# Gated S5/pooling step: chunk groups of 64, 64, 69, 69 for 69, 69, 64, 64, and two shared PSUM banks for the state-space products

## Chip, core and metric

The kernel runs on one core of one Trainium2 chip. The metric is device time in microseconds (us) of one execution; shorter is better.

## The reference, cut to what matters

Prompt (16 meta tokens and 2,048 new ones) and sample (8 sequences of 8 tokens) go through one hybrid layer, all in float32:

```
xn   = rmsnorm(h, norm_gain)
u_s, z_s, u_p, z_p, gates = split(xn @ w_in)           # six blocks of 1024
y_s  = S5 state-space branch of u_s: per group of 16 channels a complex diagonal
       recurrence s[t] = abar*s[t-1] + bbar*u[t] (64 states), y = Re(c*s) + d*u,
       gelu, then y * sigmoid(y @ w_glu + b_glu)
y_p  = causal window means (2, 4, 8, 16) of u_p minus u_p, mixed per window group
merged = g_s * ((y_s * silu(z_s)) @ w_branch_ssm) + g_p * ((y_p * silu(z_p)) @ w_branch_pool)
out  = rmsnorm(h + merged @ w_out, final_norm_gain)
```

The final states of both branches are outputs too.

## The kernel before, in words

**Tiling.** Features lie on the 128 partitions (8 blocks of 128), tokens along the free axis. T = 8 consecutive tokens are a chunk; 258 prompt chunks and 8 sample chunks make 266. They are cut into four groups (`GROUPS`) of 69, 69, 64 and 64 chunks, g0 to g3. A group has C = 8 x chunks columns, 552, 552, 512, 512. In g0 two of the chunks hold the meta tokens; only the units `us` and `up` work on them (`meta=True`), all other units of g0 have D = 536 columns. A group over 512 columns is worked in two halves (`nh` = 2), since a matmul's output is at most 512 columns wide.

**Units.** A unit is one 128 x 1024 weight block against one group (`proj`). Each float32 operand is split into a high and a low part; for each of 8 k steps a unit issues three matmuls (`mm3`, lines 129, 131 and 133: high by high, high weight by low operand, low weight by high operand) for each half: 24 matmuls of 512 columns where `nh` is 1, 48 of 268 or 276 where it is 2. ACT makes the high part of each weight block (L106) and DVE the low part (`wl`, L207) two units ahead. What is done with a unit's result (`post`) runs one unit later on ACT and DVE.

**Order of the units.** Written out by hand: us of g1 (8 units), us of g0 (8), u_pool of g0 (8 up, 8 zp, 3 gates, 4 half-sized mixes), u_pgate of g0 (13), zs of g0 (3), us of g2 (8), zs of g0 (2), us of g3 (8), zs of g0 (3), two gates, then u_rest of g0 (glu, split of the product `a`, gate, brs, gates, out), then for g1, g2 and g3 each u_pool, u_pgate, zs and u_rest. Beside the first 39 units runs the preparation of the state-space matrices (`BESIDE`: `params`, then `batches`): DVE, POOL, ACT and some small PE work, the tiles bt, ct, ps_bt and ps_k, at fixed places between matmuls.

**State-space branch.** The products run on 32 pairs of channel groups in two rounds: round 0 over the chunks of g0 and g1 (138), round 1 over those of g2 and g3 (128). A tick advances a software pipeline by one pair: its EARLY steps are issued a quarter of the way into a unit (or a part of it), its LATE steps at the end. On tick n, EARLY has st_out of pair n-6 (ACT reads `sy`, SP stores `ys`), st_turn_a and st_turn_v of pair n-2 (ACT and DVE read `sx`), st_swap, st_turn_g, st_state (POOL), st_phase, st_wrap, st_mat (SP loads `smc`); LATE has st_sin, st_rot, st_scan, st_y of pair n-5 (PE writes `sy` from `su`, `sS`, `smc`), st_x of pair n-1 (PE writes `sx` from `su`, `smb`) and st_load (SP). `sx` and `sy` are one PSUM tile each, so that st_x of a pair must wait until the reads of the pair before it, in the same tick's EARLY, are done; likewise st_y.

`spread` places the 38 ticks of a round evenly over a range of units, with a lower share in units named `busy`: round 0 from the start of u_pgate of g0 to the end of us of g3, round 1 from the glu of g0 to the end of u_pgate of g2. `a_split` of all 8 feature blocks (4 or 8 in one unit) follows the last glu of a group: 8 DVE subtractions on L115 one behind the other.

In round 1 the last 8 columns are the sample sequences; their start states are loaded beside `su` in st_load and copied by POOL into `sS` in st_state.

All DMAs are issued by SP, in program order.

Of the kernel before, what the change touches and what calls it, by code (L numbers as in the profile page):

```python
# [20 lines left out]
P = 128  # L21
DM = 1024
NB = DM // P
T = 8
KP = (2048 + 16) // T
NS = 8
# [8 lines left out]
RK = (2.0 * DM) ** (2.0 / 3.0)  # L35


GROUPS = [(0, 69), (69, 69), (138, 64), (202, 64)]
GOFF = [T * k0 for k0, _ in GROUPS]

ROUNDS = [(0, 138), (138, 128)]


W_US, W_ZS, W_UP, W_ZP, W_GS, W_GP, W_GLU, W_BRS, W_BRP, W_OUT = range(0, 80, 8)
# [45 lines left out]
def hybrid_step(ctx, tc, a):  # L90
# [388 lines left out]
    def two(q):  # L479
        return slice(2 * q, 2 * q + 2)  # L480
# [3 lines left out]
        return rows.rearrange("(q c) t k -> (c t) q k", q=2)  # L484

    def st_load(g, q):
        x = stile("su", 5, g.kn + (NS if g.last else 0))
        u = x[:, :, :g.kn]
        for i in (2 * g.i, 2 * g.i + 1):
            k = GROUPS[i][0] - ROUNDS[g.i][0]  # L490
            SY.dma_start(u[:, :, k:k + GROUPS[i][1]], chans(us_d[i], q))
        if g.last:
            SY.dma_start(x[:, :, g.kn:], a["s0"][:, 0, two(q)])
        mb = stile("smb", 2, P)
        SY.dma_start(mb, mat_d[q, :, 0])
        pr[q].update(u=u, mb=mb, s0=x[:, :, g.kn:])

    def st_phase(g, q):
        ph, n = stile("sph", 4), stile("scc", 4)
# [17 lines left out]
    def st_x(g, q):  # L517

        d = pr[q]
        d["px"] = sw["sx"][:, :, :g.kn]  # L520
        for j in range(2):
            PE.matmul(d["px"][:, j], d["mb"][:, j], d["u"][:, j], start=True, stop=True)  # L522

# [51 lines left out]
    def st_state(g, q):  # L575

        d = pr[q]
        c, w, kp = d["c"], d["s"], g.kp
        s = stile("sS", 3, g.kn)
        now = state[:, two(q)].unsqueeze(2)  # L580
        if g.last:
            G.tensor_copy(s[:, :, kp:], d["s0"])
        G.tensor_copy(s[:, :, 0:1], now)
        G.tensor_tensor(s[:, :, 1:kp], c[:, :, 1:kp], w[:, :, 1:kp], ALU.subtract)
        G.tensor_tensor(now, c[:, :, kp:kp + 1], w[:, :, kp:kp + 1], ALU.subtract)
        d["S"] = s

    def st_y(g, q):
        d = pr[q]
        d["py"] = sw["sy"][:, :, :g.kn]  # L590
        for j in range(2):
            m = slice(j * P, (j + 1) * P)
            PE.matmul(d["py"][:, j], d["m"][:, 0, m], d["u"][:, j], start=True, stop=False)  # L593
            PE.matmul(d["py"][:, j], d["m"][:, 1, m], d["S"][:, j], start=False, stop=True)  # L594
# [40 lines left out]
    class Group:  # L635
# [42 lines left out]
        def proj(self, w, xh, xl, halves=None, meta=False):  # L678


            ps = self.acc()
            n = self.HD if halves else self.ND
            nk = len(xh)
            for k in range(nk):
                between(k / nk)
                outs, xs = [], []
                for h in halves or range(self.nh):
                    m = n + (T * self.km if meta and h else 0)
                    outs.append(ps[:, h, :m])
                    xs.append([v[k][:, h * n:h * n + m] for v in (xh, xl)])  # L690
                mm3(outs, [x[:, k * P:(k + 1) * P] for x in w], xs, k == 0, k == nk - 1)
            return ps
# [63 lines left out]
        def rms_sum(self, ss, halves=None, early=False):  # L756

            n = self.HD if halves else ss.shape[1] // self.nh
            if early:
                ps = [psb.tile([P, 512], F32, tag=t, name=t)[:, :n] for t in ("bx", "by")]  # L760
            else:
                acc = self.acc()
                ps = [acc[:, h, :n] for h in range(self.nh)]
            for h in halves or range(self.nh):
                PE.matmul(ps[h], onesm, ss[:, h * n:(h + 1) * n], start=True, stop=True)  # L765
            self.ps = ps
# [54 lines left out]
        def up_post(self, fb, ps):  # L821
# [6 lines left out]
                es = E[:, :, 2 + kp:].rearrange("p t (s k) -> p t s k", k=3)  # L828
                G.tensor_copy(es[:, :, :, 0:2], self.hs.pop(fb))
            if last:  # L830
                src = ps[:, 0, :self.N].rearrange("p (t k) -> p t k", k=kn)
                A.activation(E[:, :, 2:2 + kp], src[:, :, :kp], AF.Copy)
                A.activation(es[:, :, :, 2:3], src[:, :, kp:].unsqueeze(3), AF.Copy)
            else:
                for dst, src in self.parts(E[:, :, 2:2 + kp], ps):
                    A.activation(dst, src, AF.Copy)  # L836
# [243 lines left out]
    grp = [Group(i) for i in range(NG)]  # L1080
    rounds = [Round(i) for i in range(len(ROUNDS))]
    units, events, parts, ticks, late = [], {}, {}, {}, {}

    def at(i, f, *args):
        events.setdefault(max(i, 0), []).append((f, args))
# [59 lines left out]
    def u_rest(g, nxt, ahead):  # L1145

        for f in range(NB):
            i = add("w", W_GLU + f, g.glu, f)
        for f in range(NB):
            at(i + 1 + (f // 4 if ahead == 0 else 0), g.a_split, f)  # L1150
        for f in range(ahead, 3 if ahead else 2):
            add("w", W_GS + f, g.gate, f, 0)
        ahead = 3 if ahead else 2
        for f in range(NB):
            b = add("w", W_BRS + f, g.brs, f)
            if nxt:
                at(b, nxt.x_load, f)
            if f >= NB - 2:
                at(b + 1, g.m_split, f)
            if f + ahead < NB:  # L1160
                i = add("w", W_GS + f + ahead, g.gate, f + ahead, 0)
                if f + ahead == NB - 1:
                    last_gs = i
        for j in range(NB - 2):
            at(max(last_gs + 1 + j // 3, 0), g.m_split, j)


        n = NB if nxt else NB - 3
        for f, h in [(f, None) for f in range(n)] + [(f, h) for h in range(2) for f in range(n, NB)]:
            i = add("w", W_OUT + f, g.out, f, h)  # L1170
            at(i - 2, g.r_load, f, g.cols(h))
            if nxt:
                if f == 0:
                    at(i, nxt.rs_load)
                if f >= 2 and f < 6:
                    at(i, nxt.x_norm, 2 * f - 4)
                    at(i, nxt.x_norm, 2 * f - 3)
        if nxt:
            at(i + 2, g.norm)
            for k in range(NB):  # L1180
                at(i + 3 + k, g.final, k)
            return
        at_part(i - 2, 0.5, lambda: g.rms_sum(g.ss, [0]))
        at_part(i - 2, 1.0, lambda: g.rms(g.ss, [0]))
        for k in range(NB):
            at(i - 1 + (0, 0, 0, 1, 1, 2, 2, 2)[k], g.final, k, 0)
            if k in LAST_GAIN:
                at(i, g.last_gain, k)
        at_part(i, 1.0, g.last_sum)
        at(i + 2, g.last_norm)  # L1190
        at(i + 3, g.last_final)

    def spread(r, lo, hi, busy, low):

        share = [low if i in busy else 1.0 for i in range(lo, hi)]
        total, done, n = sum(share), 0.0, 0
        for i, w in zip(range(lo, hi), share):
            done += w
# [25 lines left out]
    def to_ssm():  # L1224
        while beside():
            pass
        sw["g"] = ctx.enter_context(tc.tile_pool(name="gp", bufs=1))
        sw["p"], sw["end"] = pool("sw")
        ps = ctx.enter_context(tc.tile_pool(name="ps", bufs=1, space=PSUM))
        for n in ("sx", "sy"):  # L1230
            sw[n] = ps.tile([P, 2, 160], F32, name=n)

    def end_ssm():
        final_states()
# [225 lines left out]
```

## Time and profile before

| | |
|---|---|
| median of 3 runs | 2083.03 us (2082.71 to 2084.15) |
| the profiled execution | 2081.01 us, of which the span from first to last instruction is 2079.2 us |
| PE busy | 2041.4 us, 98% of the span, 13,024 matmuls |
| DVE, ACT, POOL busy | 1315.7, 1002.8, 547.7 us (63%, 48%, 26%) |
| PE share of the chain that ended last | 73% |
| mean granted TensorE clock | 0.996 |

The busy shares are means over stages with different limits. PE's clock is at its full level in nearly all of the span, so the time is the length of PE's stream of matmuls and of its waits.

### The profile page before, as it was taken

What the parts mean: (1) busy time and instruction counts of PE and PEld (TensorE: products, weight loads), DVE (VectorE), ACT (ScalarE), POOL (GpSimd) and SP (SyncE); (2) the same over time, 40 slices, a digit from 0 to 9 for tenths busy, and PEclk for the clock granted to TensorE, in tenths of its full rate; (3) what the DMA queues carried; (4) which work ended last, traced back from release to release, by engine and by line L of the source; (5) the groups of instructions that cost most, each with busy time, mean ns of one, the idle gap of its engine ahead of it and who ended that gap; (6) DMA issues with size and microseconds to landing.
All of it is one profiled execution on the core that took longest, in us unless ns stands there. A gap on an engine that the chain in (4) does not pass through costs nothing.

```text
span 2079.2 us, 33846 instructions
## 1 busy us (share of the span) xinstructions
PE 2041.4 (98%) x13024; PEld 1852.7 (89%) x13024; DVE 1315.7 (63%) x1848; ACT 1002.8 (48%) x1597; POOL 547.7 (26%) x716
## 2 busy tenths in 40 slices
PE   8999999999999999999999999999999999999998
PEld 8999899978999999999999998888888888888887
DVE  7789958898645776555764686535534676354444
ACT  5335469877446553366575653333432433243322
POOL 1156516574411430022332340012200200021001
PEclk9999999999999999999999999999999999999999
DMA  5446657587534643245445544334333443343233
GB/s 204 140 127 182 177 168 213 159 244 199 154 96 146 172 134 119 97 124 137 120 121 153 166 137 140 97 119 144 107 117 117 138 148 102 101 130 103 92 106 97
DMA packets 230466, 288.16 MB, mean 139 GB/s; under 512 B 115872, under 2 KB 160544, under 8 KB 230304
## 3 DMA queue, kind: packets, MB, share of 16 engines
q1 hardware_dynamic: 230304, 285.99, 45.9%
q8 instruction: 103, 1.69, 0.3%
q14 instruction: 59, 0.48, 0.1%
HBM read 242.61 MB, written 40.95 MB: 136 GB/s over the span
## 4 chain that ended last, share of the span: by engine, by line
PE 73%; DVE 1%; ACT 0%; DMA 0%; issue 0%; DVEq 0%; POOL 0%; ACTq 0%; POOLq 0%
PE acc L131 24%; PE acc L133 24%; PE acc L129 24%; PE sy L593 1%; PE sy L594 1%; PE sx L522 1%; DVE al L115 0%; DMA ys<-sS 0%; PE acc L765 0%; ACT wh L106 0%; DVE xr L1070 0%; DVE G L999 0%; DVE sg L998 0%; DVE wl L207 0%; DVE G L1017 0%
## 5 line engine op out<-in xcount | busy, mean ns | idle before, releaser
L129 PE MATMUL acc<-ah,wh 128*128 128x276 f32 (+4 forms) x3864 | 1047.5, 325 | 7.8 <-DVE po L798 3.3
L131 PE MATMUL acc<-al,wh 128*128 128x276 f32 (+4 forms) x3864 | 1040.7, 323 | 1.4 <-DVE al L115 0.7
L133 PE MATMUL acc<-ah,wl 128*128 128x276 f32 (+4 forms) x3864 | 1037.2, 322 | 1.2 <-DVE wl L207 1.2
L106 ACT ACTIVATE wh<-raw 128x1024 fp32r<-128x1024 f32 (+1 forms) x336 | 347.1, 1034 | 797.0 <-PE acc L131 502.9
L129 PEld LDWEIGHTS acc<-ah,wh 128*128 128x128 f32 x3864 | 647.6, 189 | 70.5 <-issue 4.4
L131 PEld LDWEIGHTS acc<-al,wh 128*128 128x128 f32 x3864 | 648.6, 189 | 58.2 <-DVE al L115 1.4
L133 PEld LDWEIGHTS acc<-ah,wl 128*128 128x128 f32 x3864 | 646.1, 188 | 55.3 <-DVE wl L207 1.8
L207 DVE TENSOR_TENSOR wl<-raw,wh 128x1024 fp32r<-128x1024 f32 (+1 forms) x336 | 420.8, 1253 | 126.9 <-ACT wh L106 126.3
L545 POOL TENSOR_TENSOR sXw<-sXw,sph 128x276 f32<-128x276 f32 (+1 forms) x64 | 50.1, 783 | 337.3 <-ACT sXw L531 337.2
L889 DVE SCALAR_TENSOR_TENSOR H<-H,acc 128x512 f32<-128x512 f32 (+2 forms) x64 | 44.9, 702 | 79.5 <-ACT H L888 79.5
L987 DVE SCALAR_TENSOR_TENSOR H<-po,H 128x512 f32<-128x512 f32 (+2 forms) x32 | 23.5, 733 | 113.3 <-ACT po L985 113.3
L115 DVE TENSOR_TENSOR al<-H,ah 128x512 fp32r<-128x512 f32 (+2 forms) x104 | 78.8, 790 | 14.9 <-ACT ah L106 14.0
L541 DVE TENSOR_TENSOR sX<-sx,scc 128x276 f32<-128x276 f32 (+1 forms) x64 | 27.0, 421 | 94.4 <-ACT sX L534 69.2
L963 POOL TENSOR_SCALAR w<-w 128x512 f32<-128x512 f32 (+2 forms) x32 | 28.7, 898 | 214.0 <-ACT w L962 213.8
L106 ACT ACTIVATE ah<-H 128x512 fp32r<-128x512 f32 (+2 forms) x88 | 50.9, 602 | 55.9 <-DVE H L919 39.6
L553 DVE TENSOR_TENSOR_SCAN sX<-r,state,sX 128x138 f32<-128x138 f32 (+1 forms) x128 | 73.0, 611 | 2.3
L1028 POOL TENSOR_TENSOR ss<-ss,po 128x512 f32<-128x512 f32 (+2 forms) x25 | 41.5, 1661 | 116.7 <-ACT po L1024 102.8
L853 DVE TENSOR_TENSOR w<-E 128x497 f32<-128x497 f32 (+2 forms) x32 | 23.6, 739 | 70.5 <-ACT E L836 49.5
L940 DVE SCALAR_TENSOR_TENSOR G<-sg,acc 128x512 f32<-128x512 f32 (+2 forms) x32 | 22.4, 701 | 72.0 <-PE acc L133 69.8
L844 POOL COPY hist<-E 128x16 f32<-128x16 f32 x24 | 14.1, 585 | 201.2 <-ACT E L836 201.0
L104 POOL TENSOR_SCALAR ah<-G 128x512 fp32r<-128x512 f32 (+2 forms) x16 | 15.1, 948 | 182.4 <-DVE sg L998 146.4
L998 DVE SCALAR_TENSOR_TENSOR sg<-sg,acc 128x512 f32<-128x512 f32 (+2 forms) x32 | 22.4, 700 | 63.1 <-PE acc L133 63.1
(239 smaller groups left out, 2203.9 us busy)
## 6 DMA issues: line engine op xcount, KB each, us to landing
raw<-in_wb SPq DMA_DIRECT2D x318, 512.0 KB, 3.6
smc<-mat_d SPq DMA_DIRECT2D x64, 256.0 KB, 3.6
smb<-mat_d SPq DMA_DIRECT2D x64, 128.0 KB, 2.6
H<-in_xb SPq DMA_DIRECT2D x22, 256.0 KB, 4.0
xr<-in_xb SPq DMA_DIRECT2D x19, 256.0 KB, 3.8
H<-in_xb SPq DMA_DIRECT2D x16, 276.0 KB, 5.3
us<-po SPq DMA_DIRECT2D x16, 276.0 KB, 4.3
su<-us SPq DMA_DIRECT2D x64, 69.0 KB, 3.1
```

Source lines behind the costliest of these rows:

```text
L106: A.activation(out, in_, AF.Copy)
L115: V.tensor_tensor(l, x, h.bitcast(F32), ALU.subtract)
L129: PE.matmul(out, wh, xh, start=first, stop=False)
L131: PE.matmul(out, wh, xl, start=False, stop=False)
L133: PE.matmul(out, wl, xh, start=False, stop=last)
L207: V.tensor_tensor(l[:, c], r[:, c], h[:, c].bitcast(F32), ALU.subtract)
L541: V.tensor_tensor(d["x"], d["px"][:, :, :g.kp], d["c"][:, :, 1:g.kp + 1], ALU.mult)
L545: G.tensor_tensor(d["xw"], d["xw"], d["s"][:, :, 1:g.kp + 1], ALU.mult)
L553: V.tensor_tensor_scan(x[:, j], r8[:, i].to_broadcast([P, g.kp]), x[:, j], state[:, i], ALU.mult, ALU.add)
L889: V.scalar_tensor_tensor(self.v3(out), self.v3(out), 1.0, self.pv(ps), ALU.add, ALU.mult)
L963: G.tensor_scalar(q, q, 0.044715, 1.0, ALU.mult, ALU.add)
L1028: (G if h is None else V).tensor_tensor(self.ss[:, c], self.ss[:, c], s, ALU.add)
```

## The change

Four things change. The groups are 64, 64, 69, 69 chunks, so that g0 and g1 have 512 columns (g0 496 without the meta chunks; `nh` = 1) and g2 and g3 have 552 (`nh` = 2); round 0 then has 128 chunks, round 1 138. The two PSUM tiles become two banks: in round 0 a pair's x and y products share bank q mod 2, so that consecutive pairs use different banks; in round 1 bank 0 holds x and bank 1 holds y, as before. Units at which a_split is issued (`full`) get no tick. The sample's start states are loaded by DMA straight into `sS` in st_state, and POOL's copy goes. The rest adapts places that assumed which groups have halves.

```diff
-GROUPS = [(0, 69), (69, 69), (138, 64), (202, 64)]
+GROUPS = [(0, 64), (64, 64), (128, 69), (197, 69)]
-ROUNDS = [(0, 138), (138, 128)]
+ROUNDS = [(0, 128), (128, 138)]
...
     def st_load(g, q):
-        x = stile("su", 5, g.kn + (NS if g.last else 0))
-        u = x[:, :, :g.kn]
+        u = stile("su", 5, g.kn)
...
-        if g.last:
-            SY.dma_start(x[:, :, g.kn:], a["s0"][:, 0, two(q)])
...
+    def bank(g, q, y):
+        if g.kn <= P:
+            return sw["b"][q % 2][:, 2 * y:2 * y + 2, :g.kn]
+        return sw["b"][y].rearrange("p (j a) k -> p j (a k)", j=2)[:, :, :g.kn]
...
-        d["px"] = sw["sx"][:, :, :g.kn]
+        d["px"] = bank(g, q, 0)
...
         if g.last:
-            G.tensor_copy(s[:, :, kp:], d["s0"])
+            SY.dma_start(s[:, :, kp:], a["s0"][:, 0, two(q)])
...
-        d["py"] = sw["sy"][:, :, :g.kn]
+        d["py"] = bank(g, q, 1)
...
-                    m = n + (T * self.km if meta and h else 0)
+                    m = n + (T * self.km if meta and h == self.nh - 1 else 0)
...
             if last:
-                src = ps[:, 0, :self.N].rearrange("p (t k) -> p t k", k=kn)
-                A.activation(E[:, :, 2:2 + kp], src[:, :, :kp], AF.Copy)
-                A.activation(es[:, :, :, 2:3], src[:, :, kp:].unsqueeze(3), AF.Copy)
+                tn = T // self.nh
+                for h in range(self.nh):
+                    ts, src = slice(h * tn, (h + 1) * tn), ps[:, h, :self.N].rearrange("p (t k) -> p t k", k=kn)
+                    A.activation(E[:, ts, 2:2 + kp], src[:, :, :kp], AF.Copy)
+                    A.activation(es[:, ts, :, 2:3], src[:, :, kp:].unsqueeze(3), AF.Copy)
...
         for f in range(NB):
             at(i + 1 + (f // 4 if ahead == 0 else 0), g.a_split, f)
+            full.add(i + 1 + (f // 4 if ahead == 0 else 0))
...
-        share = [low if i in busy else 1.0 for i in range(lo, hi)]
+        share = [0.0 if i in full else low if i in busy else 1.0 for i in range(lo, hi)]
...
-        for n in ("sx", "sy"):
-            sw[n] = ps.tile([P, 2, 160], F32, name=n)
+        sw["b"] = [ps.tile([P, 4, P], F32, name=f"sb{i}") for i in range(2)]
```

## Rows read from the trace of the kernel before

**Rows 1.** The page's head and busy times: us, share of the span, instructions.

```profile
span 2079.2 us, 33846 instructions
...
PE 2041.4 (98%) x13024; PEld 1852.7 (89%) x13024; DVE 1315.7 (63%) x1848; ACT 1002.8 (48%) x1597; POOL 547.7 (26%) x716
```

**Rows 2.** PE's waits: waiting line, releaser: us in total, times, longest.

```profile
PE sx L522 <- DVE sX L541: 5.4, 3, 2.8
PE sy L593 <- DMA smc<-mat_d: 4.7, 3, 2.4
...
PE ps_k L411 <- DVE ct L399: 2.6, 1, 2.6
...
PE acc L129 <- DVE H L889: 1.7, 1, 1.7
...
PE sy L593 <- ACT sS L599: 1.7, 3, 0.9
```

**Rows 3.** Busy time by window: length, PE, PEld, DVE, ACT, POOL, clock, DMA share, GB/s.

```profile
540.00:604.00 64.00, 64.00 (x524) 64.00 (x524) 35.80 (x39) 26.89 (x38) 17.33 (x14) 1.00 0.40 117
780.00:880.00 100.00, 100.00 (x790) 100.00 (x788) 60.10 (x91) 33.90 (x52) 5.00 (x11) 1.00 0.34 107
1900.00:2000.00 100.00, 100.00 (x433) 80.83 (x432) 37.55 (x43) 28.64 (x35) 3.50 (x4) 1.00 0.31 97
290.00:380.00 90.00, 85.96 (x696) 84.76 (x695) 73.25 (x117) 79.25 (x146) 52.19 (x81) 1.00 0.64 188
...
140.00:260.00 120.00, 115.63 (x1017) 109.23 (x1015) 116.72 (x142) 58.08 (x94) 74.30 (x71) 0.99 0.63 174
...
340.00:360.00 20.00, 20.00 (x167) 20.00 (x166) 15.46 (x24) 18.98 (x35) 11.61 (x17) 1.00 0.80 245
```

**Rows 4.** PE's groups by line and shape: count, busy us, mean ns, idle before.

```profile
L129 PE MATMUL acc<-ah,wh 128*128 128x512 f32 x1256 | 495.9, 395 | 0.0
...
L129 PE MATMUL acc<-ah,wh 128*128 128x276 f32 x1280 | 270.5, 293 | 2.7 <-DVE po L798 1.8 <-ACT wh L106 0.9
...
L129 PE MATMUL acc<-ah,wh 128*128 128x268 f32 x1152 | 250.9, 290 | 5.0 <-DVE al L115 2.0 <-DVE H L889 1.7 <-DVE po L798 1.4
...
L131 PE MATMUL acc<-al,wh 128*128 128x284 f32 x128 | 37.6, 294 | 0.0
...
L129 PE MATMUL acc<-ah,wh 128*128 128x256 f32 x48 | 13.6, 283 | 0.0
...
L131 PE MATMUL acc<-H,wh 128*128 128x512 f32 x32 | 12.6, 395 | 0.0
```

**Rows 5.** DVE's groups between 140 and 260 us: count, busy us, mean ns.

```profile
L207 DVE TENSOR_TENSOR wl<-raw,wh 128x1024 fp32r<-128x1024 f32 (+1 forms) x16 | 27.1, 1695 | 0.0
L389 DVE TENSOR_TENSOR bt<-bt,t 128x512 f32<-128x512 f32 x15 | 21.1, 1409 | 1.6
...
L382 DVE TENSOR_TENSOR bt<-b,tT 128x512 f32<-128x512 f32 x15 | 10.2, 682 | 0.0
L853 DVE TENSOR_TENSOR w<-w 128x425 f32<-128x425 f32 x6 | 6.4, 1066 | 0.2
...
L857 DVE TENSOR_TENSOR w<-w 128x552 f32<-128x552 f32 x1 | 0.7, 732 | 0.0
```

**Rows 6.** Timeline around the split of g0's product: DVE, then PE.

```profile
615.33 6.21 DVE L115 TENSOR_TENSOR al<-H,ah 128x536 fp32r<-128x536 f32 x8
...
621.92 0.71 PE L522 MATMUL sx<-su,smb 128*128 128x128 f32 x4 [2.82 <-DVE sX L541]
```

**Rows 7.** DVE's read of the x product in round 1, with what ended the idle time.

```profile
L541 DVE TENSOR_TENSOR sX<-sx,scc 128x240 f32<-128x240 f32 x32 | 13.0, 405 | 69.2 <-ACT sX L534 69.2
```

**Rows 8.** The page's DMA issues: count, KB each, us to landing.

```profile
smc<-mat_d SPq DMA_DIRECT2D x64, 256.0 KB, 3.6
```

**Rows 9.** Timeline of DVE behind the last matmuls: one of its steps.

```profile
2070.72 0.42 DVE L139 SCALAR_TENSOR_TENSOR sg<-sg 128x256 f32<-128x256 f32 x1 [0.56 <-ACT sg L138]
```

More of the change, by code (lines that the diff above doesn't have):

```diff
@@ L491, in st_load @@
             SY.dma_start(u[:, :, k:k + GROUPS[i][1]], chans(us_d[i], q))
-        if g.last:
-            SY.dma_start(x[:, :, g.kn:], a["s0"][:, 0, two(q)])
         mb = stile("smb", 2, P)
         SY.dma_start(mb, mat_d[q, :, 0])
-        pr[q].update(u=u, mb=mb, s0=x[:, :, g.kn:])
+        pr[q].update(u=u, mb=mb)
+    def bank(g, q, y):
+        if g.kn <= P:
+            return sw["b"][q % 2][:, 2 * y:2 * y + 2, :g.kn]
+        return sw["b"][y].rearrange("p (j a) k -> p j (a k)", j=2)[:, :, :g.kn]
     def st_phase(g, q):
@@ L759, in rms_sum @@
             if early:
-                ps = [psb.tile([P, 512], F32, tag=t, name=t)[:, :n] for t in ("bx", "by")]
+                ps = [psb.tile([P, 512], F32, tag=t, name=t)[:, :n] for t in ("bx", "by")[:self.nh]]
             else:
@@ L1082, in hybrid_step @@
     units, events, parts, ticks, late = [], {}, {}, {}, {}
+    full = set()
     def at(i, f, *args):
```

## The prediction

> **What bounds the kernel now.** I read the page's busy times first [rows 1]: PE works in 98% of the span, every other engine in 63% or less. So a microsecond counts only if it shortens PE's stream of matmuls or one of its waits. The second view is the list of PE's waits [rows 2]. The rows shown are the larger ones of the stages that the change touches: five kinds with 16.1 us together. Two of them are waits for a PSUM tile to be read: the x product waits for DVE (5.4 us in 3 waits) and the y product for ACT (1.7 us in 3). The third view, busy time by window [rows 3], says which stage is near a second limit. Between 140 and 260 us, the preparation of the state-space matrices, DVE is busy in 116.72 of 120 us while PE has waits too. Between 290 and 380 us, where round 0 runs beside u_pgate, ACT is busy in 79.25 of 90 us and DVE in 73.25. From 780 us on PE never waits for long. The change therefore acts in the first 630 us, and through the cost of a matmul of another width.
>
> **The price of a matmul by width.** A busy PE overstates a matmul, since they overlap; the distance from start to start is what counts. Three windows hold one width each [rows 3]: 64 us with 522 matmuls of 268 columns (524 less two that only reach into the window), 100 us with 788 of 276 and 100 us with 431 of 512. That is 0.1226, 0.1269 and 0.2320 us. The line through 268 and 512 has 0.448 ns a column; it gives 0.1172 for 256, 0.1298 for 284 and 0.2248 for 496, the width that the trace doesn't show. A unit of g0 then goes from 48 x 0.1226 = 5.88 to 24 x 0.2248 = 5.40 us, a unit of g1 from 6.09 to 5.57, and units of g2 and g3 from 5.57 to 6.09.
>
> **The stream.** The counts of before [rows 4], each row times three lines and the three `acc<-H` rows of 32 added: 3 x (1256 + 32) = 3864 of 512 columns, 3936 of 276, 3552 of 268, 384 of 284, 144 of 256. At these prices: 896.4 + 499.5 + 435.5 + 49.8 + 16.9 = 1898.1 us. After, by the code: g0's us and up units give 384 of 512 columns and its other units 1584 of 496, g1 1968 of 512, g2 and g3 3936 of 276 each (in g3 the last three output blocks are cut into two halves of 276 instead of 256). That is 2352 x 0.2320 + 1584 x 0.2248 + 7872 x 0.1269 = 545.7 + 356.1 + 999.0 = 1900.8. So **+2 us**, from 0 to +3: a slope of 0.52 ns, as between 268 and 276, makes 496 columns 1 ns cheaper. The columns are the same, only moved: about 18 us less PE work before u_pgate of g0 (16 units at 0.5, and 8 up, 8 zp, 3 gates and 4 half mixes at 0.49), and as much more later.
>
> **What DVE does with faster units.** This decides whether the 18 us come out where they are saved, for what is added later is always paid. Between 140 and 260 us DVE's groups [rows 5] fall in two kinds. Five rows, from wl (27.1) to bt (10.2), don't know the group's width: 80.3 us. Eleven more, from 6.4 to 0.7 us, do: 45.2. They shrink by 40 of 536 columns, 7.5%, so by 3.4 of the 125.5 us that overlap to 116.72: DVE frees 3.2 us. PE's work in that window holds 697 of these matmuls, 348 pairs that lose 2 x 0.1226 - 0.2248 = 0.020 us each: 7.1 us. With DVE already full and PE waiting for it 2.6 and 1.7 us there [rows 2], the window shrinks by DVE's 3.2 us only: **+3.9 us**. Bounds: 0, if DVE falls behind without holding PE up, and 7.1, if nothing of it comes out. I take the middle value, for DVE is busy in 97% of that window.
>
> In round 0, 13 units of u_pgate and 5 of zs lose 0.49 us each. ACT's 79.25 of 90 us [rows 3] would stand against some 84, its own part that knows the width being small; that is 94%, still below full. But one slice of 20 us has it at 18.98 already, and g2's sums of squares there grow by 8%. **+1 us**, from 0 to +8 (the whole 18 x 0.49 less nearly nothing).
>
> **The two banks.** With consecutive pairs in different banks, x of a pair needs the reads of the pair two before it, a whole tick earlier. That takes 5.4 - 2.8 = 2.6 us of waits for DVE and the 1.7 us for ACT: **-4.3 us**, bounds 0 and -4.3. What is late next is the load of `smc`: 4.7 us of waits in round 0 [rows 2], for a load that takes 3.6 us [rows 8] and is issued three quarters of a unit before its use. In the us units of g2 and g3 these three quarters grow from 4.2 to 4.6 us, in u_pgate they shrink from 4.4 to 4.05, still above 3.6. I count 3 x 0.4: **-1 us**, bounds -4.7 and +4.
>
> **No ticks beside the split.** In the timeline [rows 6] DVE works 6.21 us at the eight low parts of g0's product; the tick's DVE read of x stands behind them, and PE waits 2.82 us for it. Without a tick in that unit the wait goes: **-2.8 us**. The three ticks' worth of work falls to other units of round 1, where PE doesn't wait. Bounds: 0, if brs then waits for the same low parts, and -3.2.
>
> **At nothing.** The start states' DMA in st_state replaces one in st_load and a POOL copy; it is issued a tick before y needs it, in round 1, whose 38 ticks are spread over two groups' units, and what stands behind it on SP are weight loads that are two units ahead. If that cover went, each of 32 ticks could cost up to one landing, 3.6 us by the nearest row [rows 8]; I see nothing that takes it. The sixteen more small ACT copies of g3's up units lie under matmuls. At the end a chain of some ten DVE and ACT steps like the 0.42 us one [rows 9] runs on 276 instead of 256 columns: +0.3 us. At the start the first loads and splits are 7% smaller, worth as much the other way.
>
> **Sum.** +2 + 3.9 + 1 - 4.3 - 1 - 2.8 = -1.2 us. The profiled execution, 2081.0 us (span 2079.2 and 1.8 around it), becomes 2079.8; it lies 2.0 below the median of the runs, so the forecast for the median is 2083.0 - 1.2, rounded **2082 us**.
>
> **Rivals.** *Faster.* DVE's fullness doesn't bind: it may fall behind by a unit or two and catch up where the preparation ends, without PE noticing. Then the 3.9 us go, and with roomier us units all 4.7 us of `smc` waits: -1.2 - 3.9 - 3.7 = -8.8, 2074 us. For it: in 120 us with DVE 97% full PE met only the two waits of 2.6 and 1.7 us. Against: they show that the backlog already reaches PE.
>
> *Slower.* ACT becomes the bound of round 0 in u_pgate and zs. Its place is 290 to 400 us, its price the 8.8 us by which PE's units there got shorter, since the us units of g2 and g3 pay theirs back anyway; 1 us is counted, so +7.8: 2090 us. It decides from the point where ACT's 79.25 us reach the shortened 84 us, some 6% more work or ill placed waits. For it: the slice at 18.98 of 20. Against: the mean of 88%.
>
> *The banks don't separate.* If a bank is guarded as a whole, sharing it between x and y couples them. In round 1 DVE's read of x waits 69.2 us in all for ACT's last read of the same tile [rows 7], so readers of one tile do stand in line. Here y of one pair and x of another lie in one bank; y's write would then also wait for DVE's read of x. The reads are a tick earlier, so this bites only if DVE is a tick late; if it does, the 4.3 us come back: 2086 us. The Trainium skill, "PSUM — Partial Sum Buffer", section "PSUM bank collisions raise a hardware error", asks for just that guard, by bank and not by address, reads against reads included. By that rule the time would be this rival's if DVE were late; rows 7 agree with it as far as readers go.
>
> **How the numbers follow.** About 0.2%, 4.2 us, is what a measurement of this kernel can tell from no change. The forecast has 0.44, the faster rival 0.30, the slower one 0.20, the bank one 0.06. The two outer cases, 2074 and 2090, with 2 us of the stream's bounds beside each, make the range 2072 to 2092; left out are a round 0 that loses to ACT and to `smc` at once, and a gain beyond all named waits. The forecast's own range is 2079 to 2087. Faster by over 0.2%: 0.30. Within: the forecast's 0.44 and half of the bank case, 0.46 with rounding. Slower: 0.24.
>
> **What would show it.** In the profile of the changed kernel: 496-column matmuls at 0.225 us from start to start; in the window of the matrix preparation DVE still full and PE's waits up by 3 to 4 us; no waits of x for DVE and of y for ACT in round 0; `smc` waits near 3.5 us; no wait of x behind the split of g0's product; ACT below 95% in u_pgate. Wrong would make me: a DVE backlog that PE never meets, ACT or the loads of round 0 as a new bound, or a wait on the start states in round 1.

## The result: 0.6% slower

The changed kernel takes 2095.95 us (median of 4 runs, 2094.70 to 2099.02), the kernel before 2083.59 us (4 runs, 2082.71 to 2084.99): a ratio of 1.0063, 95% interval 1.0051 to 1.0076. That is 12.4 us more; the prediction said 2082 us and 2072 to 2092. The profiled execution of the changed kernel took 2096.09 us, its span is 2094.0.

The head of its page and PE's line of busy time stand against [rows 1]:

```profile
span 2094.0 us, 33660 instructions
...
PE 2049.5 (98%) x12950; PEld 1863.9 (89%) x12950; DVE 1312.9 (63%) x1845; ACT 1006.0 (48%) x1598; POOL 527.5 (25%) x684
```

PE is busy 8.1 us more, and the share is the same 98%. This page alone doesn't tell where the time went. The list of PE's waits does a part of it; it answers to [rows 2]:

```profile
PE sb L597 <- DMA smc<-mat_d: 9.7, 5, 3.8
PE acc L129 <- DVE po L802: 4.1, 3, 2.1
PE acc L133 <- DVE wl L207: 3.6, 5, 1.3
PE acc L129 <- DVE H L895: 3.0, 1, 3.0
PE acc L129 <- DVE al L115: 3.0, 1, 3.0
PE ps_k L411 <- DVE ct L399: 2.7, 1, 2.7
PE acc L129 <- DVE H L925: 1.5, 1, 1.5
...
PE sb L526 <- DVE sX L545: 0.7, 2, 0.5
```

(`sb` are the two shared banks; L526 is the x product, L597 the y product.) The x product's waits for DVE fell from 5.4 to 0.7 us, the y product's for ACT are gone, and so is the wait behind the split of g0's product. In their place the y product waits 9.7 us for `smc`, where it waited 4.7.

The most telling view is busy time by window when the windows are cut where a unit begins, not at round times. I counted the matmuls (24 or 48 of a unit, 12 or 24 of a mix) and cut at the first one of units 0, 8, 16, 39, 52, 73, 108 and at the last. Units 0 to 7 are us of g1, 8 to 15 us of g0, 16 to 38 u_pool of g0 beside the preparation of the SSM matrices, 39 to 51 u_pgate of g0 beside ticks, 52 to 72 zs of g0 with us of g2 and g3, 73 to 107 the rest of g0, the others g1 to g3. The columns are those of [rows 3]. First the kernel before, cut in this way:

```profile
7.83:67.86 60.03, 54.34 (x392) 52.22 (x393) 47.40 (x91) 29.38 (x47) 5.91 (x4) 0.97 0.51 176
67.86:118.89 51.03, 49.70 (x385) 49.01 (x385) 40.99 (x85) 18.53 (x40) 16.41 (x9) 1.00 0.49 155
118.89:277.99 159.10, 154.73 (x1331) 148.18 (x1330) 139.24 (x166) 75.60 (x122) 86.53 (x86) 0.99 0.61 170
277.99:378.28 100.29, 96.02 (x775) 94.43 (x773) 77.02 (x120) 83.35 (x150) 54.08 (x85) 1.00 0.62 180
378.28:536.16 157.88, 150.51 (x868) 129.99 (x866) 131.81 (x206) 117.79 (x218) 80.25 (x120) 1.00 0.72 208
536.16:756.75 220.59, 217.77 (x1782) 217.43 (x1780) 144.34 (x190) 122.11 (x195) 68.73 (x90) 1.00 0.48 136
...
756.75:2068.23 1311.48, 1311.07 (x7474) 1155.18 (x7472) 727.19 (x974) 552.30 (x823) 232.94 (x318) 1.00 0.40 121
```

and the changed kernel:

```profile
7.16:64.71 57.55, 50.20 (x196) 37.29 (x197) 44.65 (x85) 27.86 (x45) 5.49 (x4) 0.97 0.51 181
64.71:113.64 48.93, 47.00 (x192) 37.03 (x193) 40.66 (x85) 17.85 (x33) 14.74 (x8) 0.97 0.49 150
113.64:268.53 154.89, 147.40 (x826) 118.18 (x824) 136.61 (x165) 73.94 (x113) 91.89 (x87) 0.97 0.61 174
268.53:365.25 96.72, 88.52 (x461) 74.47 (x460) 74.07 (x121) 81.58 (x149) 50.58 (x84) 1.00 0.61 185
365.25:527.20 161.95, 156.46 (x1136) 151.00 (x1134) 132.03 (x212) 118.64 (x221) 72.77 (x121) 0.98 0.71 206
527.20:729.54 202.34, 201.62 (x943) 169.66 (x941) 139.12 (x190) 120.55 (x195) 62.47 (x82) 1.00 0.51 145
...
729.54:2082.11 1352.57, 1351.73 (x9174) 1270.73 (x9173) 737.67 (x972) 561.80 (x840) 226.56 (x294) 1.00 0.39 118
```

Read the lengths against each other. These are windows of one execution of each kernel, whose spans are 14.8 us apart; the medians are 12.4 apart. From unit 73 to the last matmul the changed kernel needs 1554.91 us instead of 1532.07, 22.8 more. PE is busy nearly without a gap there in both, so what the longer units of g2 and g3 cost beyond what g0 and g1 still save is paid in full. The shorter units have to earn it before unit 73, and they don't. At the prices per matmul of the prediction the units save 8.1 us up to unit 16 (8 x 0.52 and 8 x 0.49), 10.3 from 16 to 39, 6.4 from 39 to 52: 24.8. The lengths of the windows fell by 4.6, 4.2 and 3.6: 12.4. Half of the saving never came out. From 52 to 73 the 16 units of g2 and g3 and 5 of g0 cost 5.9 us more by price, and the window grew by 4.1.

In the third window DVE is busy in 88% with both kernels. PE is idle for 7.5 us instead of 4.4, and its granted clock is 0.97 instead of 0.99: it stands at the lower level, 1.2 GHz, for 10.2 us instead of 3.4, which is worth half of the difference, 3.4 us of matmul time. Together that is 6.5 us, close to the 6.1 by which the window misses its price. In the fourth window, at full clock in both, PE is idle for 8.2 instead of 4.3 us.

### The profile page after: what moved, and what is told of

It is laid out like the page before. It is cut to its first block, busy times and chain, and to the rows that moved or that the text cites. A ratio compares the mean times of both kernels' runs of the same rounds, so it can differ in the third digit from the quotient of the medians.

```text
span 2094.0 us, 33660 instructions
## 1 busy us (share of the span) xinstructions
PE 2049.5 (98%) x12950; PEld 1863.9 (89%) x12950; DVE 1312.9 (63%) x1845; ACT 1006.0 (48%) x1598; POOL 527.5 (25%) x684
## 4 chain that ended last, share of the span: by engine, by line
PE 80%; DVE 7%; issue 5%; POOL 3%; ACT 2%; DMA 2%; SPq 0%; DVEq 0%; POOLq 0%; ACTq 0%
PE acc L129 26%; PE acc L133 26%; PE acc L131 26%; DVE wl L207 1%; PE sb L597 1%; PE sb L598 1%; PE sb L526 1%; DMA mat_d<-mp 1%; DVE al L115 1%; POOL sS L588 1%; POOL sph L504 1%; POOL sXw L549 1%; ACT ah L106 0%; DVE ct L393 0%; DVE w L859 0%
## 5 line engine op out<-in xcount | busy, mean ns | idle before, releaser
L129 PE MATMUL acc<-ah,wh 128*128 128x276 f32 (+2 forms) x3840 | 1054.4, 328 | 13.3 <-DVE po L802 4.1
L133 PE MATMUL acc<-ah,wl 128*128 128x276 f32 (+2 forms) x3840 | 1040.2, 324 | 3.7 <-DVE wl L207 3.6
L131 PE MATMUL acc<-al,wh 128*128 128x276 f32 (+2 forms) x3840 | 1041.6, 324 | 1.1 <-DVE al L729 0.6
L549 POOL TENSOR_TENSOR sXw<-sXw,sph 128x256 f32<-128x256 f32 (+1 forms) x64 | 46.9, 732 | 337.8 <-ACT sXw L535 337.8
L895 DVE SCALAR_TENSOR_TENSOR H<-H,acc 128x552 f32<-128x552 f32 (+2 forms) x64 | 44.9, 702 | 81.4 <-ACT H L894 81.4
L115 DVE TENSOR_TENSOR al<-H,ah 128x552 fp32r<-128x552 f32 (+2 forms) x104 | 77.4, 777 | 14.7 <-ACT ah L106 13.8
L969 POOL TENSOR_SCALAR w<-w 128x552 f32<-128x552 f32 (+2 forms) x32 | 28.6, 893 | 228.4 <-ACT w L968 228.2
L106 ACT ACTIVATE ah<-H 128x552 fp32r<-128x552 f32 (+2 forms) x88 | 50.9, 602 | 55.7 <-DVE H L925 39.5
L557 DVE TENSOR_TENSOR_SCAN sX<-r,state,sX 128x128 f32<-128x128 f32 (+1 forms) x128 | 75.5, 629 | 2.3
L1034 POOL TENSOR_TENSOR ss<-ss,po 128x552 f32<-128x552 f32 (+2 forms) x25 | 41.8, 1672 | 115.9 <-ACT po L1030 115.9
L850 POOL COPY hist<-E 128x16 f32<-128x16 f32 x24 | 14.7, 612 | 194.0 <-ACT E L842 193.7
```

What stands on the lines that cost most here:

```text
L106: A.activation(out, in_, AF.Copy)
L115: V.tensor_tensor(l, x, h.bitcast(F32), ALU.subtract)
L129: PE.matmul(out, wh, xh, start=first, stop=False)
L131: PE.matmul(out, wh, xl, start=False, stop=False)
L133: PE.matmul(out, wl, xh, start=False, stop=last)
L549: G.tensor_tensor(d["xw"], d["xw"], d["s"][:, :, 1:g.kp + 1], ALU.mult)
```

## The experiments

Each time is a median; the kernel before, run on the same chip, had 2084.86 us in the first four, 2083.82 in the next four, 2084.06 in the next four and 2084.44 in the last three. The changed kernel's 2095.95 us was taken beside 2083.59, so differences between kernels of unlike groups are less sure, by about 1 us, than the intervals given.

**All of the change but the groups.**

```diff
-GROUPS = [(0, 64), (64, 64), (128, 69), (197, 69)]
-ROUNDS = [(0, 128), (128, 138)]
+GROUPS = [(0, 69), (69, 69), (138, 64), (202, 64)]
+ROUNDS = [(0, 138), (138, 128)]
```

> The changed kernel with the groups of before (69, 69, 64, 64; rounds of 138 and 128): the banks, the ticks left out beside the split and the start states' DMA stay; since 138 chunks don't fit, only round 1 has two banks in turn. Theory A (the regrouping costs all of it): about 3 us below the kernel before, 2080 to 2081 us, the 2.8 us wait of x behind the split of g0's product gone and all else as before. Rival B (banks, ticks or the start states' DMA cost too): 2085 us or more.

2080.94 us, 0.9981 of before (0.9972 to 0.9991). So the other edits together gain 3.9 us, and the regrouping costs 12.4 + 3.9 = 16.3. The rest of the runs look for those.

**The changed kernel with the kinds of products in a bank each**, as before (the two lines that put both kinds in one bank taken out of the function that gives the bank).

> The changed kernel with x in bank 0 and y in bank 1 in round 0 too, so that consecutive pairs share a bank again. Theory A (the banks only exchange one wait for another, the load of smc): within 3 us of the changed kernel, 2093 to 2099 us, with PE's waits of x for DVE and of y for ACT back at 3 to 5 us and its waits for smc down by as much. Rival B (the banks took 4 us as forecast, and the regrouping alone brought the smc waits): 2099 to 2101 us with the smc waits unchanged at 9.7 us.

2096.70 us (1.0058, 1.0043 to 1.0073), 0.7 us from the changed kernel, with four runs of each that spread over 3 to 4 us. Its list of waits:

```profile
PE sb L595 <- ACT sS L601: 4.9, 3, 2.5
PE sb L524 <- DVE sX L543: 3.5, 4, 2.6
...
PE sb L595 <- DMA smc<-mat_d: 1.9, 2, 1.1
```

The PSUM waits are back with 8.4 us, and the wait for `smc` has fallen to 1.9. The two banks take one wait away and give another of the same size (10.3 us of the three kinds here, 10.4 in the changed kernel). The likely reading is that a y product that comes earlier meets its load earlier.

**The loads of `smc` issued later**, at the end of the tick before, behind the loads of `su` and `smb`:

```diff
-             (4, st_state), (0, st_phase), (1, st_wrap), (4, st_mat))
+             (4, st_state), (0, st_phase), (1, st_wrap))
-    LATE = (..., (1, st_x), (0, st_load))
+    LATE = (..., (1, st_x), (0, st_load), (3, st_mat))
```

> The changed kernel with the load of smc issued at the end of a tick's LATE steps, two ticks before its use, instead of behind the store of ys in the next tick's EARLY steps, where SP waits for ACT. Theory A (what is late in round 0 is this load, because of what stands ahead of it on SP): PE's 9.7 us of waits for smc fall below 2 us, the stretch at half the clock behind the one of 3.8 us goes with them, and the time falls by 8 to 13 us to 2083 to 2088 us. Rival B (ACT or DVE is the bound of round 0): the waits move to other releasers and the time stays above 2092 us.

2094.94 us (1.0051, 1.0036 to 1.0066), within 1 us of the changed kernel. In the profiled execution, the longest of the four with 2098.43 us, the waits for `smc` are gone, and again others stand there:

```profile
PE sb L526 <- DMA smb<-mat_d: 7.5, 6, 3.0
...
PE sb L598 <- POOL sS L588: 1.5, 1, 1.5
```

So this load isn't what is late by itself: with it out of the way the next inputs of the tick make PE wait. A theory that names this one load falls.

**Filler matmuls against TensorE's clock.** In the changed kernel four waits of some 3 us before unit 73 are each followed by 3 to 7 us in which the granted clock is half, 1.2 GHz; the kernel before has one such wait there. (Each has one more such stretch, of 3.4 us, near 33 us.) Eleven more matmuls were put into the preparation's wait for `ct` and 15 ahead of one y product:

```diff
+                for _ in range(11 if b == 13 and i == 0 else 0):
+                    PE.matmul(pk[:, 3], ident, ident, start=True, stop=True)
...
+        for _ in range(15 if q == 16 and not g.last else 0):
+            PE.matmul(d["py"][:, 0], d["u"][:, 0, :P], d["u"][:, 0], start=True, stop=True)
```

> The changed kernel with extra matmuls of no use inside two waits of PE: 11 of 128 columns (two passes each) ahead of the wait for ct in the fourteenth batch of the matrix preparation (2.7 us) and 15 ahead of the wait for smc of pair 16 in round 0 (3.8 us). They write PSUM that is written again before it is read. Theory A (PE's clock falls to 1.2 GHz behind a wait in which PE does nothing, and the loss of 3.4 us behind each of these two comes on top of the waits): no half clock from 233 to 240 us and from 414 to 421 us, and 5 to 7 us less than the changed kernel, 2089 to 2091 us, although PE does more. Rival B (the clock falls for another reason, or what it loses would be waited for anyway): 2094 us or more.

2095.57 us (1.0054, 1.0039 to 1.0069): nothing gained. Busy time by window, around the two places that were filled:

```profile
228.00:246.00 18.00, 16.94 (x108) 13.52 (x108) 17.61 (x23) 9.20 (x15) 10.65 (x10) 1.00 0.60 163
405.00:425.00 20.00, 19.38 (x161) 19.19 (x160) 17.61 (x30) 15.88 (x35) 12.07 (x21) 1.00 0.84 262
```

The clock stays full there, so the half clock does follow the idle PE. Another stretch grew: from 183.60 to 190.40 us the granted clock is 0.50, and a new one of 3.4 us stands near 358 us. Between 113 and 527 us PE is at half clock for 10.2 us, where it was 17.1. Unit 39 begins only 0.9 us earlier (267.60), and unit 73 0.8 (526.39). So two of the stretches were taken out, not all, and the run bounds what the clock costs by itself rather than showing that it costs nothing.

**The short group at another place.** Two kernels with the same widths, only the first two groups changed in their order. All the other edits are the changed kernel's.

```diff
-GROUPS = [(0, 64), (64, 64), (128, 69), (197, 69)]
-ROUNDS = [(0, 128), (128, 138)]
+GROUPS = [(0, 64), (64, 69), (133, 64), (197, 69)]    # g0 short
+GROUPS = [(0, 69), (69, 64), (133, 64), (197, 69)]    # g1 short
+ROUNDS = [(0, 133), (133, 133)]
```

> The changed kernel with groups of 64, 69, 64, 69 chunks and rounds of 133 and 133 (so the banks are given by kind of product, as in the second round of the changed kernel). Beside its sister run (69, 64, 64, 69) only the first two groups change places. Theory (the loss is made where group 0's units run beside the preparation of the SSM matrices and the first SSM ticks: VectorE and the queues set the pace there, so shorter units of TensorE give nothing, while the longer units of groups 2 and 3 are paid in full later): group 0 is short here, so most of the loss stays: 2089 to 2094 us, and unit 39 (the first of group 0's pool branch products) starts within 4 us of the changed kernel's 268.5 although group 1's eight first units are about 4 us longer. Rival (the loss comes from unlike rounds, 128 against 138, or from the two-banks rule, wherever the short group stands): both sister runs come out alike, 2082 to 2088.

> The changed kernel with groups of 69, 64, 64, 69 chunks and rounds of 133 and 133. Theory (loss made in group 0's units): group 1 is the short one, with only eight units in the early stretch and the other 73 of them later where TensorE alone sets the pace, so nearly all of it is gained back: 2081 to 2086 us, and unit 39 starts between 272 and 278. Rival (unlike rounds or the banks): the same time as the run with 64, 69, 64, 69, within 2 us.

2100.42 us (1.0080, 1.0065 to 1.0095) with g0 short, 2083.90 (0.9998, 0.9989 to 1.0008) with g1 short. The same widths in another order differ by 16.5 us. Some 2.8 of them are the price of the units themselves, since a unit of g0 saves 0.49 us and one of g1 0.52; the rest is what doesn't come out. The direction is that of the theory, but the first lies 6 us beyond its range. Busy time by window between units 39 and 52 and between 52 and 73, g0 short:

```profile
269.97:369.54 99.57, 90.72 (x461) 75.00 (x460) 76.36 (x122) 82.42 (x150) 52.69 (x85) 1.00 0.64 188
369.54:532.60 163.06, 153.84 (x941) 136.83 (x940) 132.72 (x209) 117.63 (x219) 75.12 (x120) 0.99 0.71 203
```

and with g1 short:

```profile
276.38:375.49 99.11, 95.17 (x775) 93.94 (x773) 76.41 (x121) 83.44 (x151) 53.11 (x85) 1.00 0.63 182
375.49:539.32 163.83, 155.75 (x1062) 144.09 (x1061) 133.08 (x207) 117.50 (x218) 76.33 (x119) 0.99 0.69 201
```

The 13 units of u_pgate are 6.4 us shorter in the first kernel by price, and take as long (99.57 and 99.11 us): PE stands idle for 8.9 us instead of 3.9. From 16 to 39 the windows took 154.08 and 159.08 us, 5.0 apart where the price says 10.3. Group 0's units are the ones that don't pay.

**Less work for DVE early.** Both kernels without the addition that completes the state input matrices (16 instructions; the matrices lack one of their two terms):

```diff
-            V.tensor_tensor(d["bt"], d["bt"], d["t4"], ALU.add)
```

> The changed kernel with the addition of the second half of the state input matrices left out on VectorE (16 instructions of about 1.4 us, some 22 us of VectorE's time before unit 39; the matrices lack one of their two terms). Theory (VectorE sets the early pace in the changed kernel): unit 39 starts 6 to 10 us earlier than in the changed kernel and the end comes 5 to 10 us earlier: 2086 to 2091 us; the kernel before, with the same addition left out, gains less, 2 to 6 us. Rival (TensorE's clock or the queue of SyncE sets it): under 2 us in both.

> The kernel before with the same 16 additions left out (the matrices lack one term): Theory (its longer units leave VectorE nearly enough time): 2078 to 2082 us, a gain of 2 to 6 us, less than the changed kernel gains. Rival (the early stretch is equally bound in both): the same gain as in the changed kernel, so that the difference of 12 us between the two stays.

2085.07 us (1.0003, 0.9994 to 1.0012) for the changed kernel, a gain of 10.9; 2076.65 (0.9964, 0.9952 to 0.9977) for the kernel before, 7.2 under the 2083.82 of the same chip; both gains are some 1 us more than expected at most. The window from unit 16 to 39, changed kernel:

```profile
113.55:257.73 144.18, 142.82 (x825) 115.34 (x824) 126.39 (x150) 74.04 (x113) 88.06 (x87) 1.00 0.67 187
```

and the kernel before:

```profile
118.71:272.38 153.67, 153.31 (x1331) 147.11 (x1329) 127.93 (x150) 76.80 (x123) 82.04 (x86) 1.00 0.64 178
```

With DVE relieved the two windows are 9.5 us apart, nearly the 10.3 of the price; with its full work they were 4.2 apart. So in this stretch DVE kept about 5 us of the saving from coming out. The kernel before gains too (5.4 us in this window, the changed one 10.7): DVE held it up as well, only less. The half clock goes with DVE's work: the granted clock is 1.00 in both windows. Two things these runs leave open. The addition takes DVE's time and also stands in the chain of steps that leads to the matrices, and the runs don't tell these apart. And how much of the loss is waiting and how much is the slower clock behind the waits they don't tell either.

**Also a shorter chain in the ticks of round 0.** Both light kernels without the two ScalarE copies that swap the halves of the scanned state, in round 0 only (the unswapped state is used, so the first round's states are other numbers):

```diff
+        if not g.last:
+            d["xw"] = d["x"]
+            return
         z, zw = d["x"], stile("sXw", 2, g.kp)
```

> The changed kernel without the 16 additions on VectorE (as in the run before) and, in the first SSM round, without the two ScalarE copies that swap the halves of the scanned state (64 copies of 0.42 us; the unswapped state is used instead, and the first round's states are other numbers). Theory (beside group 0's pool branch products the chain of each SSM tick over ScalarE, VectorE and GpSimd sets the pace, so the shorter units give little there): with 0.8 us less in each pair's chain the 13 units from unit 39 shorten from 96.4 to 91 to 94 us, the end comes 2 to 5 us earlier than with the additions alone left out: 2080 to 2083 us, and its distance to the kernel before with the same two cuts falls from 8.4 to 3 to 7 us. Rival (SyncE's queue of loads sets it): the wait for smc stays at 9 to 11 us, the gain is under 1 us, the distance stays 8 to 9 us.

> The kernel before with the same two cuts. Theory: its longer units hide most of the chain already: a gain of 0 to 2 us over the run with the additions alone left out, 2074.5 to 2077 us. Rival: as large a gain as in the changed kernel.

2083.63 us (0.9998, 0.9987 to 1.0009) and 2079.73 (0.9979, 0.9969 to 0.9989). The distance fell to 3.9 us, but not for the reason given: the changed kernel gained 1.4 us only, and the other 3.1 come from the kernel before, which was slower with less work. Neither theory had that, and the cause stays open. This pair decides nothing.

**Fewer ticks in the 13 units of u_pgate**, in the changed kernel:

```diff
+        if r is rounds[0]:
+            share[:13] = [0.75] * 13
         total, done, n = sum(share), 0.0, 0
```

> The changed kernel with a share of 0.75 instead of 1 for the 13 pool branch units of group 0 in the spreading of the first round's ticks: about 13 ticks there instead of 16, and the others spread over the 21 units behind them, eight of group 2 and eight of group 3, which are the longer ones. Theory A (too many ticks for the shortened units is all that is wrong there): the 13 units shorten by 2 to 3 us, the later ones hide the added ticks, and the end comes 2 to 3 us earlier, 2092.5 to 2094 us. Theory B (the work of the ticks as a whole binds the round): what the 13 units gain the later ones lose, the same time within 1.5 us.

2091.39 us (1.0034, 1.0022 to 1.0045), 4.6 less than the changed kernel, more than the theory gave. From unit 16 to 39, 39 to 52 and 52 to 73:

```profile
113.60:268.91 155.31, 147.32 (x828) 117.30 (x827) 135.98 (x165) 73.75 (x113) 92.46 (x87) 0.98 0.61 174
268.91:352.91 84.00, 83.18 (x424) 70.97 (x425) 63.64 (x100) 71.96 (x125) 41.36 (x66) 1.00 0.63 192
352.91:522.88 169.97, 161.32 (x1171) 154.18 (x1170) 142.22 (x233) 126.38 (x244) 84.92 (x139) 0.99 0.70 208
```

The 13 units take 84.0 us instead of 96.7, and PE is idle for 0.8 us of them instead of 8.2. The units behind take 8.0 more. 4.7 us of the two together are gone for good.

**The edit at the split alone**, on the kernel before:

```diff
+            full.add(i + 1 + (f // 4 if ahead == 0 else 0))
...
-        share = [low if i in busy else 1.0 for i in range(lo, hi)]
+        share = [0.0 if i in full else low if i in busy else 1.0 for i in range(lo, hi)]
```

> The kernel before with one part of the change alone: no ticks in the units that hold the split of the SSM branch's operand. Theory: the wait of 2.8 us of TensorE for the product from the first product's bank, near 622 us of the kernel before, goes and nothing takes its place: 2080 to 2081.5 us, the same as the kernel with all but the groups. Rival (the two banks of the second round or the start states make the gain of that kernel): the same as before, 2083 to 2084.5 us.

2080.07 us (0.9979, 0.9969 to 0.9989): 4.0 us gained, as with all of the change but the groups (3.9). The window from unit 73 to 108 is down from 220.59 to 217.50 us, with PE busy in all of it:

```profile
534.74:752.24 217.50, 217.50 (x1782) 217.37 (x1781) 142.82 (x190) 121.95 (x195) 68.15 (x90) 1.00 0.49 139
```

**Fewer ticks on the old groups, and with less DVE work.** Three kernels with the share of 0.75: the kernel before with the edit at the split, and the two without the additions.

> The kernel before with no ticks beside the split, and with the share of 0.75 for the 13 pool branch units. Theory (the ticks crowd those units only once they are shortened: 13 units of 6.1 us hold 16 ticks where 13 of 5.6 us do not): little left to gain here, 0 to 1.5 us under the kernel with the split alone, 2078.5 to 2080.5 us. Rival (the 13 units are crowded at either length, so their shortening is not what lost the time): as much as in the changed kernel, 4 to 5 us, 2075 to 2076 us.

> The changed kernel without the 16 additions on VectorE (matrices lack one term) and with the share of 0.75. Theory (two separate losses, early on VectorE and in the 13 units): the two gains of 10.9 and 4.6 us add up: 2079 to 2082 us. Rival (one loss seen at two places): the sum falls short by 3 us or more, 2083 to 2085 us.

> The kernel before with the same two edits. Theory: 0 to 1.5 us under the one without the additions alone, 2075 to 2077 us, so that the distance of the changed kernel falls from 12.4 to 8.4 (additions) to 3 to 6 us (both). Rival (crowded at either length): 2071 to 2073 us, the distance stays near 8 us.

2079.57 us (0.9970, 0.9960 to 0.9980), 2079.94 (0.9978, 0.9968 to 0.9987) and 2074.92 (0.9953, 0.9938 to 0.9968). On the old groups fewer ticks gain 0.5 and 1.7 us; on the new ones 4.6 and 5.1. So the crowd in u_pgate belongs to the shortened units. And the gains add up: the changed kernel stands 12.4 us behind the kernel before, 8.4 when DVE has less to do, 5.0 when its 13 units also hold fewer ticks. What makes up the last 5.0 wasn't taken apart. The first of the three is the fastest kernel here that computes the whole reference, 0.3% under the kernel before; it can't be told from the edit at the split alone.

## Why the prediction was wrong

**The step that failed** is the one on what DVE does with faster units: +3.9 us was counted and 8.9 were lost. The prediction saw the right thing: the 18 us count only where PE alone sets the pace, and DVE is full there. It then sized the loss too small. It looked at the window from 140 to 260 us alone, took from it the middle of its bounds, 3.9 of 7.1 us, and let the rest of the 18 us come out. Of those 18.4 us 9.5 arrived at unit 39 (268.53 against 277.99), so 8.9 were lost. Some 6 of them lie between unit 16 and 39 (10.3 by price, 4.2 measured). The forecast sign, PE's waits up by 3 to 4 us in the preparation, did come (3.1 us more idle time); what it had no term for are the stretches at half clock behind such waits, 10.2 us of them instead of 3.4. The runs with less DVE work show DVE as the cause of about 5 of the 6 us, by waiting and clock together. The other 3 or so lie ahead of unit 16, where the prediction counted nothing; PE's waits for DVE's `al` and `wl` there are 5.7 us instead of 3.2 before. What makes them wasn't tried. The half clock there isn't it alone: without the 16 additions the changed kernel happened to spend 3.4 us less at half clock ahead of unit 16, and reached it at 113.55 us instead of 113.64.

**u_pgate and zs.** +1 us was counted, bounds 0 to 8. The 13 units of u_pgate alone lost 2.8 of 6.4 us, and the 21 units behind them took 1.8 less than their price: 0.9 or 1 us lost in all. That the number came true is partly luck: the prediction didn't reckon with the ticks' own products, which became narrower in this round, 128 columns for 138, and fewer ticks in the 13 units give back 4.6 us of the time, 3 to 4 more than on the old groups. It isn't ACT as a full engine, as the slower rival had it: ACT is busy in 81.58 of 96.72 us, 84%. That rival's 2090 us was the nearest number, by a mechanism that the runs don't bear out. Which engine or queue orders the ticks' chain there stays open: moving the load of `smc` changed nothing, and two copies less gave 1.4 us.

**A second step failed by as much: the two banks.** -4.3 us was counted, and -1 for the loads. The waits named did go (5.4 to 0.7 and 1.7 to 0 us), but the wait for `smc` went up by 5.0 us in place of down, and the kernel without the shared bank took the same time. The net is 0, as far as four runs of each can tell; 4.3 us would have shown. The prediction reckoned the lead of that load from the length of a unit, 4.2 to 4.4 us against 3.6 to land. By that there should have been no wait for `smc` in the kernel before either, and there were 4.7 us of it. The rival that the banks don't separate is wrong as told: the waits of x for DVE did go. The coupling that it names does exist, at a small price: in the changed kernel with fewer ticks in u_pgate a y product waits 0.6 us for DVE's read of the x product in its bank. The rule of the Trainium skill, "PSUM — Partial Sum Buffer", section "PSUM bank collisions raise a hardware error", is to guard PSUM by bank and not by address; in these runs it cost PE no more than that.

**A term that the prediction lacks.** The x and y products of round 1 went from 128 to 138 columns, in a stretch where PE alone sets the pace. From start to start their 384 records in the trace take 43.7 us behind unit 73, where they took 40.1: 3.6 us, paid in full, while the narrower products of round 0 lie where PE waits.

**What held.** A matmul of 496 columns: from 179.73 to 180.41 us the timeline has three from start to start, 0.227 us each (0.225 forecast; the median of 829 such distances behind 500 us is 0.225):

```profile
179.73 0.39 PE L133 MATMUL acc<-H,wl 128*128 128x496 f32 x1
179.96 0.39 PE L129 MATMUL acc<-H,wh 128*128 128x496 f32 x1
180.18 0.39 PE L131 MATMUL acc<-H,wh 128*128 128x496 f32 x1
180.41 0.39 PE L133 MATMUL acc<-H,wl 128*128 128x496 f32 x1
```

The edit at the split: -2.8 forecast, -4.0 us measured alone, an interval of 2.3 to 6.5 that holds the forecast. The start states' transfers cost nothing seen: from unit 108 on PE is busy in 1351.73 of 1352.57 us.

**The sum with the sizes measured**, for the two profiled executions: +2.7 for the stream at the forecast prices (1900.8 less 1898.1), +8.9 lost before unit 39, +0.9 between 39 and 73, +1.3 from there to the last matmul (3.6 for the wider products, some 3 off for the split, and 0.7 that no run explains), and +0.9 behind it, where 0.3 was forecast: 14.7 of the 14.8 us between the spans. The medians are 12.4 us apart because the profiled execution of before, 2081.01 us, lies 2.6 under its median. The banks and loads stand at 0 in this sum.

## What to carry to other kernels

Before moving work from one stage to another, cut the profile at the program's units and ask of each stage whether the engine that gets lighter is the one that sets its pace: a saving where another engine is full is worth a fraction, while its price where TensorE runs alone is paid whole. Here a long group 0 belongs first: with the other edits kept, the groups 69, 69, 64, 64 took 2080.94 us and 69, 64, 64, 69 took 2083.90, but 64, 64, 69, 69 took 2095.95 and 64, 69, 64, 69 took 2100.42. A wait that goes away on a list of waits is a gain only if the total of that list falls; look at what the freed instruction needs next.

## Unexpected of the hardware

TensorE's clock fell behind single waits in a stage in which it works in 147.40 of 154.89 us. After 3.04 us of waiting for DVE, at 185.34 us, the matmuls of 512 columns come 0.43 us apart instead of 0.23, and they do so until 188.8 us:

```profile
185.34 0.66 PE L129 MATMUL acc<-ah,wh 128*128 128x512 f32 x1 [3.04 <-DVE H L895]
185.79 0.63 PE L131 MATMUL acc<-al,wh 128*128 128x512 f32 x1
186.22 0.63 PE L133 MATMUL acc<-ah,wl 128*128 128x512 f32 x1
```

In busy time by window the granted clock of that stretch is 0.52, about the lower level of 1.2 GHz, and back at 0.99 behind it:

```profile
185.40:188.60 3.20, 3.20 (x8) 2.55 (x9) 3.10 (x5) 2.31 (x4) 2.00 (x2) 0.52 0.82 217
188.80:195.00 6.20, 6.20 (x41) 4.95 (x40) 6.05 (x8) 3.60 (x6) 3.05 (x3) 0.99 0.65 155
```

One would add such stretches to the bill of a wait. For this kernel that overstates it: the run with filler matmuls took two of them out, with 6.8 us less at half clock between units 16 and 73, and the end came 0.4 us earlier, less than the noise. The likely reason is that a slower PE in part uses up time that it would have waited for DVE and the ticks. That is argued from these times and not shown, and stretches were left in that run.

The addition that the light kernels leave out takes DVE 0.69 us once and 1.40 to 1.43 us in the other 15 of its 16 places, in every run that has it. In those 15 a GpSimd product (L392) is under way when it begins; in the one it isn't. First DVE in the kernel before, then GpSimd and DVE in the changed one:

```profile
135.89 0.69 DVE L389 TENSOR_TENSOR bt<-bt,t 128x512 f32<-128x512 f32 x1
...
142.14 1.41 DVE L389 TENSOR_TENSOR bt<-bt,t 128x512 f32<-128x512 f32 x1
```

```profile
179.37 1.48 POOL L392 TENSOR_TENSOR t4b<-craw,tT 128x512 f32<-128x512 f32 x1 [1.67 <-DVE ct L399]
...
179.99 1.41 DVE L389 TENSOR_TENSOR bt<-bt,t 128x512 f32<-128x512 f32 x1
```

That is some 10.8 us (15 x 0.72, an estimate) of DVE's time in the stage that it paces. No run moved the GpSimd product away, so what it is worth stays open.
